# Side steps two at a time, block moves on two queues, and memory blocks split later, in a two-layer hybrid encoder trunk

## The chip, the core and the metric

The kernel runs on one core of a Trainium2 chip. The metric is the device time of one execution in microseconds (us). Each timed result is a median over runs of the same program; one further execution is recorded by the hardware profiler, and the rows below come from that one. The engines carry the profile's names: PE is TensorE (PEld its weight load), DVE is VectorE, ACT is ScalarE, POOL is GpSimd, SP is SyncE, which does nothing here but issue DMAs.

## The reference

x (256 tokens x 2048) goes through two layers. A layer normalizes x, projects it to 15,944 columns, and splits these into four branches of 512 columns (4 heads of 128) and their gates:

```python
h = rms_norm(x, norm_g); u = h @ w_in                                  # 2048 -> 15944
y_a = sparse_index_attention(norm(a_q), norm(a_k), a_v, a_qi, a_ki, a_wi)   # 8 index heads, top 64 keys
y_b = head_rms_norm(retention(rope(b_q), rope(b_k) * HD ** -0.5, b_v))
y_c = head_rms_norm(hgrn2(f, c_i, c_q))                               # f = lb + (1 - lb) * sigmoid(c_f)
m_k, m_v = halves of mem @ w_mem_kv                                   # mem: 256 x 2048
y_m = memory_attention(norm(m_q), norm(m_k), m_v)
merged = sum_n sigmoid(gate_n) * ((y_n * silu(z_n)) @ w_branch[n])    # 512 -> 2048, n = a, b, c, m
x = x + merged @ w_out
```

Everything is float32.

## The kernel before, in words

**The weight stream.** All weights, 336 tiles in the fixed order of `gemm_plan`, pass once through the core. A tile holds four blocks of 128 rows by (mostly) 512 columns, 1 MB. `load` has SP fetch a tile into `raw` (four buffers). `split_weights` takes half a tile (a half slab): ACT casts it to `whi` (L223), DVE subtracts to get the rest `wlo` (L224), and when a tile's second half is split, the next load is issued (L230). In `gemms` a half slab meets two blocks of the left operand, itself split into a high and a low part, in 12 products: high by high, high by low, low by high (L249 to L251) for two blocks and two halves of the 256 rows. There are 672 half slabs. Four pairs `whi`, `wlo` exist, so splits are written up to four half slabs ahead of the products.

**The side work.** Everything between the large products (norms, attention, retention, recurrence, transposes, the splitting of a left operand) is written as generators, the tasks of the class `Stream`. A `yield` ends a side step; a step that cannot go on gives BLOCKED. After the 12 products of each half slab `pump` (L113) runs at most one side step, that of the first task in line that can move. Where a product needs a task's result, `finish` (L123) runs that task to its end first, with no half slab between its steps. All this happens when the program is built: it decides the order in which each engine gets its instructions. Engines then run in that order and wait for each other by semaphores.

**The moves.** A 128 x 128 transpose is done by `fold` (L286): DVE transposes 32 x 32 blocks inside (tile names end in i), then 16 DMAs put the blocks in place, all on GpSimd's queue (L300). `tick` (L108), the first thing in `pump`, issues up to four moves per half slab; three half slabs after the last one the task goes on (L311). There are 44 such tiles, 704 moves.

**The start.** The left operand of the first 64 half slabs is the memory (mem transposed, four blocks `memr`, split to `memh` and `meml`), for the keys `mk` and values `mv` of both layers. The loop at L575 to L596 loads and splits the four blocks among the first weight tiles. The task `constants` (L603) loads the blocks of x transposed (`xr`, L613) and scales them with `split_scaled` (four activations on ACT each, L274), then loads x itself (`xs`, L619) for the norm.

**The places named below.** `bw` is a branch's product with its output weights, in the order c, a, m, b (L739); before it the branch's transposed output is cast (L266: `bnh` for c and b, `ah`, `mh`). `ixrp` are the index scores of branch a (L458), from the transposed index queries `ixqt` and keys `ixkt`. `bk` is the key of branch b, rotated on DVE in `rope_t` (L479 to L492). PSUM has two tiles for side work (`PB`) beside two for the stream.

Of the kernel before, what the change touches and what calls it, by code (L numbers as in the profile page):

```python
# [89 lines left out]
MOVES = 4  # L90


class Stream:
    def __init__(self):
        self.loaded = self.cut = self.used = self.ticks = self.idle = 0
        self.raw, self.parts, self.tasks, self.moves = deque(), deque(), [], deque()
# [10 lines left out]

    def tick(self):  # L108
        self.ticks += 1
        for _ in range(min(MOVES, len(self.moves))):  # L110
            self.moves.popleft()()

    def pump(self):  # L113
        self.tick()
        for t in list(self.tasks):
            moved = t.step()
            if t.done:
                self.tasks.remove(t)
            if moved:
                return True  # L120
        return False
# [43 lines left out]
def trunk(ctx: ExitStack, tc: tile.TileContext, x, xt, memt, ng, qkg, hg, lbl, win, wmem, wbr, wout,  # L165
# [120 lines left out]
    def fold(cuts, nb, name):  # L286
        inner = G([128, nb, 128], name + "i")
        at = 0
        for shape, src in cuts:
            n = int(np.prod(shape))  # L290
            part = inner[:, at:at + n, :]
            if len(shape) == 2:
                part = part.rearrange("p (a b) c -> p a b c", a=shape[0])
            ve.transpose(part, src)
            at += n
        yield from stream.rest(1)
        whole = G([128, nb, 128], name)

        def move(a, b):
            po.dma_start(whole[b, :, a], inner[a, :, b])  # L300

        cut = [slice(32 * i, 32 * i + 32) for i in range(4)]
        left = [(a, b) for a in cut for b in cut]

        def moved():
            move(*left.pop())

        stream.moves.extend([moved] * 16)
        while left:
            yield BLOCKED  # L310
        yield from stream.rest(3)  # L311
        return whole
# [56 lines left out]
    def head_norm(ps, zs, g, name):  # L369
        v = ps.rearrange("p (a d) -> p a d", a=8)  # L370
        zg = G([128, 2, 512], name + "zg")
        ve.tensor_tensor(zg, zs, g[:, None, :].to_broadcast([128, 2, W]), op=OP.mult)
        sq = G([128, 8, 128], name + "sq")
        ac.activation(sq, v, AF.Square)
        yield
        ss = SM(8, name + "ss")
        ve.reduce_sum(ss, sq, axis=AX.X)
        r = rsq(ss, 8, 1.0 / HD, name)
        yield
        y1 = G([128, 8, 128], name + "y1")  # L380
        ve.tensor_mul(y1, v, bc(r, HD))
        y = G([128, 2, 512], name + "y")
        ve.tensor_tensor(y, y1.rearrange("p (t h) d -> p t (h d)", t=2), zg, op=OP.mult)
        yield
        return (yield from branch_t(y, name))

    def attend(box, names, keys, name):
# [6 lines left out]
        for t in range(2):  # L394
            nk = keys[t]
            nb = nk // 128
            lg = PB(f"{name}lg{t}")[:, :4 * nk].rearrange("p (h s) -> p h s", h=4)
# [3 lines left out]
            if masks is not None:  # L401
                lm = G([128, 4, nk], f"{name}lm{t}")
                ve.tensor_add(lm, lg, masks[t][:, None, :].to_broadcast([128, 4, nk]))
                lg = lm
            mx = SM(4, f"{name}mx{t}")
# [6 lines left out]
            for h in range(4):  # L412
                ac.activation(p[:, h, :], lg[:, h, :], AF.Exp, bias=nm[:, h:h + 1], scale=ISQ,
                              accum_out=sm[:, h:h + 1])
            yield
# [5 lines left out]
            yield  # L421
            ov = PB(f"{name}ov{t}")[:, :512].rearrange("p (h d) -> p h d", h=4)
# [6 lines left out]
            ve.tensor_mul(on, ov, bc(rc, HD))  # L429
            zs = yield from wait_for(box, names[3])  # L430
# [5 lines left out]
    def selection(qi0, qi1, name):  # L436
# [11 lines left out]
        for t in range(2):  # L448
# [3 lines left out]
            for g in range(8 // per):  # L452
                yield
                ps = PB(f"{name}rp{t}{g}").rearrange("p (h s) -> p h s", h=per)
# [6 lines left out]
                ac.activation(rl, ps, AF.Relu, scale=NID ** -0.5)  # L461
                for h in range(g * per, g * per + per):
# [48 lines left out]
    def retention_scores(qt, kt, name):  # L511
        p0 = PB(name + "s0").rearrange("p (h t) -> p h t", h=4)
# [3 lines left out]
        ve.tensor_mul(s0, p0, csb[:, C_D:C_D + 1024].rearrange("p (h t) -> p h t", h=4))  # L516
        yield
        p1 = PB(name + "s1")[:, :512].rearrange("p (h t) -> p h t", h=4)
# [3 lines left out]
        ve.tensor_mul(s1, p1, csb[:, C_D + 1024:C_D + 1536].rearrange("p (h t) -> p h t", h=4))  # L522
        return (lambda h: s0[:, h, 0:128]), (lambda h: s0[:, h, 128:256]), (lambda h: s1[:, h, :])

    def hgrn_scores(uf, uq, lb, olb, name):
# [10 lines left out]
        yield  # L536
        ps = PB(name + "dg").rearrange("p (g t) -> p g t", g=8)
# [4 lines left out]
        ve.tensor_mul(a, ps, ident[:, None, :].to_broadcast([128, 8, 128]))  # L542
        tot = f.rearrange("p h t -> p (h t)")
        for i, m in enumerate(LEVELS):
            nb = 64 // m
            yield
            yield from stream.rest(1)
            ps = PB(f"{name}l{i}")[:, :512]
            for g in range(8):
# [7 lines left out]
                ps.rearrange("p (b j) -> p b j", j=m))  # L557
            tv = tot.rearrange("p (b two) -> p b two", two=2)
# [8 lines left out]
        yield  # L567
        ps = PB(name + "x")[:, :512].rearrange("p (h t) -> p h t", h=4)
# [3 lines left out]
        ac.copy(ax, ps)  # L572
        return (lambda h: a[:, 2 * h, :]), (lambda h: ax[:, h, :]), (lambda h: a[:, 2 * h + 1, :])

    memx = []  # L575
    for b in range(4):
        raw = G([128, 4, 256], "memr")
        hi = G([128, 4, 256], "memh", F32R)
        lo = G([128, 4, 256], "meml", F32R)
        for k0, k1 in [(0, 1), (1, 2), (2, 4)] if b == 0 else [(0, 4)]:  # L580
            if b == 0 and k0 == 0:
                part = load(True)
                part(0, 1)
            sy.dma_start(raw[:, k0:k1, :], memt[:, 4 * b + k0:4 * b + k1, :])
            if b == 0:
                for k in range(max(k0, 1), k1):
                    part(k, k + 1)
            ac.copy(hi[:, k0:k1, :], raw[:, k0:k1, :])
            ve.tensor_sub(lo[:, k0:k1, :], raw[:, k0:k1, :], hi[:, k0:k1, :].bitcast(F32))
            if b == 0 and k0 > 0:  # L590
                split_weights(True)
        memx.append((hi, lo))
        if stream.loaded < RAW:
            load()
        if b >= 2 and len(stream.parts) < HL:
            split_weights()  # L596
# [72 lines left out]
    for l in range(L):  # L669
# [8 lines left out]
        def mixed(scores, v, z, g, name):  # L678
# [3 lines left out]
            yield  # L682
            return (yield from head_norm(mix_values(sc, vt, name), zs, g, name + "n"))
# [37 lines left out]
        def merged(acc, d):  # L721
            if d == 3:
                yield
                u = turned_at_once(acc, "mgp")
            else:
                u = yield from transposed(acc, "mgp")
# [20 lines left out]
        def turned(c, xc, nssq, l=l):  # L747
            if c >= 2:
                yield
                u = turned_at_once(xc, "xp")  # L750
            else:
                u = yield from transposed(xc, "xp")
            r = split_scaled(u, ngs[:, l + 1, 4 * c:4 * c + 4], xtp, "xt", f"x1{c}")
            for t in range(2):
# [67 lines left out]
```

## Time and profile before

| | |
|---|---|
| timed, median of 3 runs | 1927.73 us (1927.24 to 1927.80) |
| the profiled execution | 1934.95 us, span of its instructions 1933.2 us |
| busy share: PE, DVE, ACT, POOL | 98%, 58%, 45%, 23% |
| mean granted clock of TensorE | 0.99 of 2.4 GHz |
| DMA: hardware queues, software queue (GpSimd's) | 52.8%, 5.6% of 16 engines' span |

The page cuts the span in 40 slices; a digit is the busy share, or the granted clock, in tenths:

```profile
PE   6999999999979999999999999999997999999999
PEclk8999999999989999999999999999998999999999
POOL 0323055056251001010120306406623101001000
```

TensorE is below nine tenths in slices 1, 12 and 31; its clock is lower in the same ones. A row of a timeline reads: start in us from the span's start, duration, engine, line, operation, output<-inputs, shape, count, and in brackets the idle time before it with what ended it.

### The profile page before, as it was taken

The numbers are of one execution on the slowest core, as the hardware profiler recorded it, in microseconds if no ns is written. First come the engines' busy times: TensorE is split into PE (matmuls) and PEld (weight loads), VectorE is DVE, ScalarE is ACT, GpSimd is POOL, SyncE is SP. The second block draws the span as 40 slices with busy tenths as digits, with TensorE's granted clock in tenths as the row PEclk, the third lists the DMA queues.
The fourth block names the chain that finished last, engine by engine and source line by source line (L and its number), as shares of the span: only waits on it lengthen the run. The fifth ranks groups of instructions, "written<-read, shape, count | busy, mean of one in ns | idle before, by whom it ended". The sixth has DMA issues, their size and how long they took to land.

```text
span 1933.2 us, 22621 instructions
## 1 busy us (share of the span) xinstructions
PE 1888.2 (98%) x8736; PEld 1576.7 (82%) x8736; DVE 1129.6 (58%) x1204; ACT 864.2 (45%) x995; POOL 437.6 (23%) x729
## 2 busy tenths in 40 slices
PE   6999999999979999999999999999997999999999
PEld 5888987888868888888888898888886888888887
DVE  5645765766655555555555577677564545555554
ACT  4644354445434444444454434454453444444442
POOL 0323055056251001010120306406623101001000
PEclk8999999999989999999999999999998999999999
DMA  7765556567465556565565546646755656556553
GB/s 294 264 222 174 186 189 190 191 201 210 163 182 197 191 193 204 195 206 196 188 203 207 167 173 205 212 180 204 230 167 162 202 192 204 195 196 207 195 196 110
DMA packets 76139, 379.18 MB, mean 196 GB/s; under 512 B 17536, under 2 KB 18944, under 8 KB 35072
## 3 DMA queue, kind: packets, MB, share of 16 engines
q1 hardware_dynamic: 53504, 355.94, 52.8%
q0 software_dynamic: 22528, 21.80, 5.6%
q8 instruction: 68, 1.11, 0.2%
q14 instruction: 39, 0.32, 0.1%
HBM read 353.82 MB, written 2.10 MB: 184 GB/s over the span
## 4 chain that ended last, share of the span: by engine, by line
PE 94%; DMA 3%; POOL 1%; issue 0%; DVE 0%; SPq 0%; ACT 0%; DVEq 0%; ACTq 0%; POOLq 0%
PE u L249 23%; PE u L250 23%; PE u L251 22%; PE bw L249 3%; PE bw L251 3%; PE bw L250 3%; PE wo L251 3%; PE wo L250 3%; PE wo L249 3%; PE cl L551 1%; PE mv L250 1%; PE mv L251 1%; PE mv L249 1%; DMA memr<-in_memt 1%; PE mk L251 1%; PE mk L250 1%
## 5 line engine op out<-in xcount | busy, mean ns | idle before, releaser
L224 DVE TENSOR_TENSOR wlo<-raw,whi 128x1024 fp32r<-128x1024 f32 (+2 forms) x674 | 804.1, 1198 | 670.2 <-ACT whi L223 669.2
L223 ACT CAST whi<-raw 128x1024 fp32r<-128x1024 f32 (+2 forms) x674 | 694.9, 1033 | 951.4 <-PE u L251 738.2
L300 POOL DMA_DIRECT2D mgp<-mgpi x96 | 55.2, 583 | 493.4 <-ACT whi L223 294.7
L249 PE MATMUL u<-whi,x02h 128*128 128x512 f32 (+2 forms) x256 | 99.4, 388 | 0.0
L249 PE MATMUL u<-whi,x12h 128*128 128x512 f32 (+2 forms) x256 | 99.0, 387 | 0.0
L249 PE MATMUL u<-whi,x00h 128*128 128x512 f32 (+2 forms) x256 | 98.9, 386 | 0.0
L249 PE MATMUL u<-whi,x10h 128*128 128x512 f32 (+2 forms) x256 | 98.9, 386 | 0.0
L249 PE MATMUL u<-whi,x11h 128*128 128x512 f32 (+2 forms) x256 | 98.6, 385 | 0.0
L249 PE MATMUL u<-whi,x01h 128*128 128x512 f32 (+2 forms) x256 | 98.6, 385 | 0.0
L249 PE MATMUL u<-whi,x03h 128*128 128x512 f32 (+2 forms) x256 | 98.5, 385 | 0.0
L249 PE MATMUL u<-whi,x13h 128*128 128x512 f32 (+2 forms) x256 | 98.5, 385 | 0.0
L250 PE MATMUL u<-wlo,x02h 128*128 128x512 f32 (+2 forms) x256 | 98.4, 384 | 0.0
L251 PE MATMUL u<-whi,x02l 128*128 128x512 f32 (+2 forms) x256 | 98.3, 384 | 0.0
L250 PE MATMUL u<-wlo,x12h 128*128 128x512 f32 (+2 forms) x256 | 98.2, 383 | 0.0
L251 PE MATMUL u<-whi,x12l 128*128 128x512 f32 (+2 forms) x256 | 98.2, 383 | 0.0
L251 PE MATMUL u<-whi,x11l 128*128 128x512 f32 (+2 forms) x256 | 98.2, 383 | 0.0
L250 PE MATMUL u<-wlo,x00h 128*128 128x512 f32 (+2 forms) x256 | 98.1, 383 | 0.0
L250 PE MATMUL u<-wlo,x10h 128*128 128x512 f32 (+2 forms) x256 | 98.1, 383 | 0.0
L251 PE MATMUL u<-whi,x10l 128*128 128x512 f32 (+2 forms) x256 | 98.1, 383 | 0.0
L251 PE MATMUL u<-whi,x00l 128*128 128x512 f32 (+2 forms) x256 | 98.1, 383 | 0.0
L250 PE MATMUL u<-wlo,x11h 128*128 128x512 f32 (+2 forms) x256 | 98.1, 383 | 0.0
L250 PE MATMUL u<-wlo,x13h 128*128 128x512 f32 (+2 forms) x256 | 98.1, 383 | 0.0
(369 smaller groups left out, 3883.5 us busy)
## 6 DMA issues: line engine op xcount, KB each, us to landing
raw<-in_win SPq DMA_DIRECT2D x240, 1024.0 KB, 4.9
raw<-in_wbr SPq DMA_DIRECT2D x32, 1024.0 KB, 4.8
raw<-in_wout SPq DMA_DIRECT2D x32, 1024.0 KB, 4.9
raw<-in_wmem SPq DMA_DIRECT2D x15, 1024.0 KB, 5.1
raw<-in_win SPq DMA_DIRECT2D x8, 656.0 KB, 4.0
raw<-in_win SPq DMA_DIRECT2D x8, 512.0 KB, 3.5
mgp<-mgpi POOLq DMA_DIRECT2D x96, 32.0 KB, 4.1
xr<-in_xt SPq DMA_DIRECT2D x4, 512.0 KB, 6.0
```

The source lines that it names most:

```text
L223: ac.copy(hi[:, a:b, :], r)
L224: ve.tensor_sub(lo[:, a:b, :], r, hi[:, a:b, :].bitcast(F32))
L249: te.matmul(ps[:, t, :n], ah[:, 2 * j + k, c], wh[:, k, :], start=first, stop=False)
L250: te.matmul(ps[:, t, :n], ah[:, 2 * j + k, c], wl[:, k, :], start=False, stop=False)
L251: te.matmul(ps[:, t, :n], al[:, 2 * j + k, c], wh[:, k, :], start=False, stop=last)
L300: po.dma_start(whole[b, :, a], inner[a, :, b])
L551: te.matmul(ps[:, g * 64:g * 64 + 64].rearrange("p (b j) -> p b j", j=m), kd[:, g // 2, c], qd[:, g // 2, c].rearrange("p (b two j) -> p b ...
```

## The change

After each half slab up to two side steps are taken instead of one (a task gives one step per turn, so they come from two tasks). Counters for PSUM keep two side tiles open at most: a step that would take a third is BLOCKED (`bank` ahead of each such tile, `free` behind its last reader; both act only while the program is built). Of the moves that `tick` issues, every second goes to SP's queue. At the start the loads are written ahead of the splits, one more weight tile is issued before the small loads, and memory blocks 1 to 3 are split as whole blocks by three tasks, which come up after half slabs 1, 4 and 7.

```diff
-MOVES = 4
+MOVES, STEPS, BANKS = 4, 2, 2
...
+    def bank(self):
+        while self.banks == BANKS:
+            yield BLOCKED
+        self.banks += 1
+    def free(self):
+        self.banks -= 1
     def tick(self):
         self.ticks += 1
-        for _ in range(min(MOVES, len(self.moves))):
-            self.moves.popleft()()
+        for i in range(min(MOVES, len(self.moves))):
+            self.moves.popleft()(i)
     def pump(self):
         self.tick()
+        n = 0
         for t in list(self.tasks):
-            moved = t.step()
+            n += t.step()
             if t.done:
                 self.tasks.remove(t)
-            if moved:
-                return True
-        return False
+            if n == STEPS:
+                break
...
-        def move(a, b):
-            po.dma_start(whole[b, :, a], inner[a, :, b])
+        def move(q, a, b):
+            q.dma_start(whole[b, :, a], inner[a, :, b])
...
-        def moved():
-            move(*left.pop())
+        def moved(i):
+            move((po, sy)[i % 2], *left.pop())
...
@     def retention_scores(qt, kt, name):
+        yield from stream.bank()
         p0 = PB(name + "s0").rearrange("p (h t) -> p h t", h=4)
...
         ve.tensor_mul(s0, p0, csb[:, C_D:C_D + 1024].rearrange("p (h t) -> p h t", h=4))
+        stream.free()
...
-    memx = []
-    for b in range(4):
-        raw = G([128, 4, 256], "memr")
...
+    def split_later(raw, after, name):
+        yield from stream.rest(after)
+        return split(raw, gen, "g", name)
+
+    part = load(True)
+    part(0, 1)
+    raw = G([128, 4, 256], "memr")
+    for k0, k1 in [(0, 1), (1, 2), (2, 4)]:
+        sy.dma_start(raw[:, k0:k1, :], memt[:, k0:k1, :])
+        for k in range(max(k0, 1), k1):
+            part(k, k + 1)
+    memr = [raw] + [G([128, 4, 256], "memr") for b in range(1, 4)]
+    load()
+    sy.dma_start(memr[1], memt[:, 4:8, :])
+    load()
+    load()
+    for b in (2, 3):
+        sy.dma_start(memr[b], memt[:, 4 * b:4 * b + 4, :])
+    hi = G([128, 4, 256], "memh", F32R)
+    lo = G([128, 4, 256], "meml", F32R)
+    split_pieces(hi, lo, raw, [(0, 1), (1, 2)])
+    split_weights(True)
+    split_pieces(hi, lo, raw, [(2, 4)])
+    split_weights(True)
+    split_weights()
+    split_weights()
+    memx = [(hi, lo)] + [stream.add(split_later(memr[b], 3 * b - 2, "mem")) for b in range(1, 4)]
```

What this moves on the engines, as the order of their instructions shows it:

ACT at the start, before; `memh` are casts of memory blocks, `whi` casts of weights (the first two half slabs in two pieces each), `x00h` the scaling of the first x block:

```order
L588 CAST memh<-memr 128x256 x2
L223 CAST whi<-raw 128x512 x2
L588 CAST memh<-memr 128x512
L223 CAST whi<-raw 128x512 x2
L588 CAST memh<-memr 128x1024 x2
L223 CAST whi<-raw 128x1024
L588 CAST memh<-memr 128x1024
L223 CAST whi<-raw 128x1024 x5
L274 ACTIVATE x00h<-xr,ngs 128x256 x4
```

The same place after:

```order
L604 CAST memh<-memr 128x256 x2
L231 CAST whi<-raw 128x512 x2
L604 CAST memh<-memr 128x512
L231 CAST whi<-raw 128x512 x2
L231 CAST whi<-raw 128x1024 x3
L274 CAST memh<-memr 128x1024
L231 CAST whi<-raw 128x1024 x3
L274 CAST memh<-memr 128x1024
L282 ACTIVATE x00h<-xr,ngs 128x256 x4
```

The casts of blocks 1 to 3 stand among or behind weight casts that they stood ahead of: block 1 has the weights of five half slabs ahead of it instead of two, and between block 0 and the scaling of x stand six casts of whole weight halves and two blocks instead of six and three; the last block follows the second x block.

ACT before the product of branch m in layer 0, before; `mh` is the cast of m, `bnh` that of b, `mp` the exponentials of m, each `gate` belongs to one `bw`:

```order
L223 CAST whi<-raw 128x1024
L374 ACTIVATE bnsq<-bo 128x1024
L223 CAST whi<-raw 128x1024 x5
L736 ACT_TABLE_LOAD
L736 ACTIVATE gate<-u,rs0r 128x512 x2
L223 CAST whi<-raw 128x1024 x10
L736 ACTIVATE gate<-u,rs0r 128x512 x2
L266 CAST mh<-mpt 128x1024
L266 CAST bnh<-bnpt 128x1024
L223 CAST whi<-raw 128x1024 x10
L736 ACTIVATE gate<-u,rs0r 128x512 x2
```

After, the same stretch:

```order
L231 CAST whi<-raw 128x1024 x7
L776 ACTIVATE gate<-u,rs0r 128x512 x2
L231 CAST whi<-raw 128x1024 x4
L274 CAST bnh<-bnpt 128x1024
L231 CAST whi<-raw 128x1024 x4
L274 CAST mh<-mpt 128x1024
L231 CAST whi<-raw 128x1024 x2
L776 ACTIVATE gate<-u,rs0r 128x512 x2
L231 CAST whi<-raw 128x1024 x10
L776 ACTIVATE gate<-u,rs0r 128x512 x2
```

The cast of m stood directly behind the gate of its own product, with no weight cast between; it now stands behind the cast of b, which followed it before, two weight casts ahead of the gate of branch a and twelve ahead of its own.

SP in layer 0 around the index branch, before; `raw` are weight tiles:

```order
L670 DMA hgs<-in_hg 128x1024
L211 DMA raw<-in_win 128x2048 x11
L211 DMA raw<-in_win 128x1024 x4
L211 DMA raw<-in_win 128x1312 x4
L211 DMA raw<-in_win 128x2048 x44
```

After, the stretch with the index keys `ixkt`, the output of branch c (`cnpt`) and the index queries `ixqt`:

```order
L219 DMA raw<-in_win 128x2048 x8
L308 DMA ixkt<-ixkti 32x2x32 x4
L219 DMA raw<-in_win 128x2048
L308 DMA ixkt<-ixkti 32x2x32 x4
L219 DMA raw<-in_win 128x2048
L308 DMA cnpt<-cnpti 32x8x32 x4
L219 DMA raw<-in_win 128x2048
L308 DMA cnpt<-cnpti 32x8x32 x4
L219 DMA raw<-in_win 128x2048
L308 DMA ixqt<-ixqti 32x8x32 x4
L219 DMA raw<-in_win 128x2048
L308 DMA ixqt<-ixqti 32x8x32 x4
```

SP had only weight loads there; now four moves of a tile stand between two of them, and GpSimd has the other eight of each sixteen.

## Rows read from the trace of the kernel before

**Rows 1.** the page: busy us, share of the span, instructions by engine

```profile
PE 1888.2 (98%) x8736; PEld 1576.7 (82%) x8736; DVE 1129.6 (58%) x1204; ACT 864.2 (45%) x995; POOL 437.6 (23%) x729
```

**Rows 2.** what TensorE waited for: us in total, times, longest

```profile
PE bw L249 <- ACT mh L266: 20.7, 2, 10.7
PE mv L249 <- ACT whi L223: 9.3, 1, 9.3
...
PE ixrp L458 <- DMA akpt<-akpti: 4.0, 1, 4.0
```

**Rows 3.** TensorE's timeline, layer 0, around m's product: start us, us, what

```profile
557.92 0.39 PE L249 MATMUL u<-whi,x03h 128*128 128x512 f32 x1
...
576.60 0.39 PE L249 MATMUL bw<-whi,mh 128*128 128x512 f32 x1
```

**Rows 4.** the same in layer 1

```profile
1466.31 0.39 PE L249 MATMUL u<-whi,x13h 128*128 128x512 f32 x1
...
1484.39 0.39 PE L249 MATMUL bw<-whi,mh 128*128 128x512 f32 x1
```

**Rows 5.** by stretch, third and fourth half slab: busy us, then PEclk

```profile
23.10:29.50 6.40, 5.75 (x13) 4.18 (x14) 5.92 (x6) 3.72 (x4) 0.00 (x0) 0.50 0.27 79
```

**Rows 6.** timeline, layer 0, GpSimd's moves of m and ScalarE's cast of m

```profile
563.77 3.45 POOL L300 DMA_DIRECT2D mpt<-mpti  x6 [0.16 <-issue]
570.45 1.04 ACT L266 CAST mh<-mpt 128x1024 fp32r<-128x1024 f32 x1 [7.40 <-DMA mpt<-mpti]
```

**Rows 7.** TensorE at the first index scores, layer 0, then layer 1

```profile
312.82 0.39 PE L249 MATMUL u<-whi,x01h 128*128 128x512 f32 x1
...
319.73 2.27 PE L458 MATMUL ixrp<-ixkt,ixqt 64*128 64x128 f32 x16 [4.03 <-DMA akpt<-akpti]
...
325.41 0.39 PE L249 MATMUL u<-whi,x02h 128*128 128x512 f32 x1
...
1227.05 0.39 PE L249 MATMUL u<-whi,x11h 128*128 128x512 f32 x1
...
1233.81 0.39 PE L249 MATMUL u<-whi,x12h 128*128 128x512 f32 x1
```

**Rows 8.** GpSimd's timeline, the last moves of the index queries

```profile
311.32 2.31 POOL L300 DMA_DIRECT2D ixqt<-ixqti  x4 [2.05 <-issue]
```

**Rows 9.** ScalarE's timeline at the start

```profile
10.99 0.62 ACT L223 CAST whi<-raw 128x512 fp32r<-128x512 f32 x1 [0.75 <-DMA raw<-in_wmem]
17.25 1.04 ACT L588 CAST memh<-memr 128x1024 fp32r<-128x1024 f32 x1 [5.64 <-DMA memr<-in_memt]
...
33.44 1.71 ACT L274 ACTIVATE x00h<-xr,ngs 128x256 fp32r<-128x256 f32 x4
```

**Rows 10.** TensorE's timeline, two half slabs in step

```profile
32.28 0.39 PE L249 MATMUL mk<-whi,memh 128*128 128x512 f32 x1
...
35.00 0.39 PE L249 MATMUL mk<-whi,memh 128*128 128x512 f32 x1
```

**Rows 11.** SP's issues at the start (SPq: its sequencer)

```profile
4.98 2.11 SPq L584 DMA_DIRECT2D memr<-in_memt  x1
...
45.70 0.33 SPq L211 DMA_DIRECT2D raw<-in_wmem  x1
46.07 0.65 SPq L619 DMA_DIRECT2D xs<-in_x  x1
```

**Rows 12.** the page: queues with their share; issues with us to landing

```profile
q0 software_dynamic: 22528, 21.80, 5.6%
...
mgp<-mgpi POOLq DMA_DIRECT2D x96, 32.0 KB, 4.1
xr<-in_xt SPq DMA_DIRECT2D x4, 512.0 KB, 6.0
```

**Rows 13.** VectorE's timeline around the rotation of bk

```profile
427.43 0.74 DVE L488 SCALAR_TENSOR_TENSOR bka<-u,rs0r,csb 128x512 f32<-128x512 f32 x1
...
433.14 1.22 DVE L224 TENSOR_TENSOR wlo<-raw,whi 128x1024 fp32r<-128x1024 f32 x1
```

More of the change, by code (lines that the diff above doesn't have):

```diff
@@ L404, in attend @@
                 lg = lm
+                stream.free()
             mx = SM(4, f"{name}mx{t}")
@@ L414, in attend @@
                               accum_out=sm[:, h:h + 1])
+            if masks is None:
+                stream.free()
             yield
@@ L421, in attend @@
             yield
+            yield from stream.bank()
             ov = PB(f"{name}ov{t}")[:, :512].rearrange("p (h d) -> p h d", h=4)
@@ L453, in selection @@
                 yield
+                yield from stream.bank()
                 ps = PB(f"{name}rp{t}{g}").rearrange("p (h s) -> p h s", h=per)
@@ L511, in retention_scores @@
     def retention_scores(qt, kt, name):
+        yield from stream.bank()
         p0 = PB(name + "s0").rearrange("p (h t) -> p h t", h=4)
@@ L516, in retention_scores @@
         ve.tensor_mul(s0, p0, csb[:, C_D:C_D + 1024].rearrange("p (h t) -> p h t", h=4))
+        stream.free()
         yield
+        yield from stream.bank()
         p1 = PB(name + "s1")[:, :512].rearrange("p (h t) -> p h t", h=4)
@@ L536, in hgrn_scores @@
         yield
+        yield from stream.bank()
         ps = PB(name + "dg").rearrange("p (g t) -> p g t", g=8)
@@ L547, in hgrn_scores @@
             yield from stream.rest(1)
+            yield from stream.bank()
             ps = PB(f"{name}l{i}")[:, :512]
@@ L567, in hgrn_scores @@
         yield
+        yield from stream.bank()
         ps = PB(name + "x")[:, :512].rearrange("p (h t) -> p h t", h=4)
@@ L572, in hgrn_scores, with split_pieces @@
         ac.copy(ax, ps)
+        stream.free()
         return (lambda h: a[:, 2 * h, :]), (lambda h: ax[:, h, :]), (lambda h: a[:, 2 * h + 1, :])
-    memx = []
-    for b in range(4):
-        raw = G([128, 4, 256], "memr")
[L578 to L587, printed above, removed]
+    def split_pieces(hi, lo, raw, cuts):
+        for k0, k1 in cuts:
             ac.copy(hi[:, k0:k1, :], raw[:, k0:k1, :])
             ve.tensor_sub(lo[:, k0:k1, :], raw[:, k0:k1, :], hi[:, k0:k1, :].bitcast(F32))
[L590 to L596, printed above, removed]
+    def split_later(raw, after, name):
[24 more added lines that the diff above has]
+    memx = [(hi, lo)] + [stream.add(split_later(memr[b], 3 * b - 2, "mem")) for b in range(1, 4)]
     box = {}
@@ L682, in mixed @@
             yield
+            yield from stream.bank()
             return (yield from head_norm(mix_values(sc, vt, name), zs, g, name + "n"))
@@ L723, in merged @@
                 yield
-                u = turned_at_once(acc, "mgp")
-            else:
-                u = yield from transposed(acc, "mgp")
+                yield from stream.bank()
+                r = split(turned_at_once(acc, "mgp"), gen, "g", f"mg{d}")
+                stream.free()
+                return r
+            u = yield from transposed(acc, "mgp")
             return split(u, gen, "g", f"mg{d}")
@@ L749, in turned @@
                 yield
+                yield from stream.bank()
                 u = turned_at_once(xc, "xp")
```

9 lines of the change are left out of this document (8 added, 1 removed).

## The prediction, made before the changed kernel ran

> **What bounds the kernel now.** I read the page's busy shares first, then the list of what TensorE waited for, then the timeline around each wait, and last the order of the instructions. TensorE is busy for 98% of the span [rows 1], nearly all of it in the 672 half slabs of the weight stream: 12 products each, one half slab every 2.72 us (32.28 to 35.00 in [rows 10]). That pace isn't touched by the change: it has the same products in the same number. What can be won is only where TensorE stands still or runs at its lower clock, and the list of waits has four such places [rows 2]: the start (9.28 us), the index scores of layer 0 (4.03), and the first product of branch m with its output weights in each layer (10.74 and 10.00, one row with count 2). Each costs more than the wait, since TensorE comes back at its lower level: after the wait at the start it was granted 0.50 of the clock, 1.2 of 2.4 GHz, for 6.4 us [rows 5]. So I take each loss from the first product before the wait to the first at full pace behind it.
>
> **The products of branch m, both layers: 25.9 us.** In layer 0, 24 products run from 557.92 to 576.60, 18.68 us; at full pace two half slabs take 5.44, so 13.24 are lost [rows 3]. In layer 1 it is 1466.31 to 1484.39, 18.08, so 12.64 [rows 4]. The cause stands on the other engines: the block moves of m (tile mpt) are still being issued by GpSimd at 567.2, and ScalarE waits 7.40 us for them before it can cast m [rows 6]. The program had run out of half slabs there: it issues 12 of the 16 moves, the cast and the subtraction after the last half slab before the product. In the new order the cast of m stands 12 half slabs (32.6 us) ahead of the product, in both layers, because two side steps after each half slab let m run beside the other branches. Even if its moves landed 10 us late, TensorE would not notice. What is late next there is branch b, whose cast stands 26 half slabs ahead of its product. I count the whole 25.9.
>
> **The index scores of layer 0: 5.8 us.** The half slab with them and the next take 12.59 us in layer 0 (312.82 to 325.41), and 6.76 in layer 1, where nothing is waited for (1227.05 to 1233.81): 5.83 lost [rows 7]. The wait ended with the last moves of the query tile ixqt. GpSimd was behind: at 3.45 us for six moves [rows 6] the four moves after each half slab take it 2.3 of 2.72 us, and it stood still besides, as the 2.05 us before the last four moves of ixqt show [rows 8]. Now SP issues half of them, the scores come 8 half slabs earlier in the stream, and their last moves are due for issue four half slabs (10.9 us) before them, as they were, but on two queues, neither of which lags. I count the whole 5.8.
>
> **The start: 5 us, between 0 and 11.3.** ScalarE works in order. Before, it casts memory blocks 1, 2 and 3 among the first weights, so the third half slab's weights wait behind blocks that TensorE doesn't need yet: the cast of block 1 stood 5.64 us for its landing at 17.25, and block 2 comes later still [rows 9]. Now the second weight tile's two casts come first. When does that tile land? Between 10.99 (first weights complete) and 17.25 there landed two weight tiles and block 1, 2.5 MB, so 2.5 us per MB [rows 9]. The second tile lands at 10.99 + 2.5 = 13.5, its cast takes 1.04, and the third half slab starts at 14.6 instead of 23.1. Its second product waits 1.0 for the subtraction (1.22 us, as in [rows 13]). Six half slabs later, at 14.6 + 1.0 + 16.3 = 31.9, TensorE wants half slab 8. In the kernel before it had it at 32.28 + 4 x 2.72 = 43.2 [rows 10], a lead of 11.3 us: the upper end.
> But in front of that half slab's cast stands the scaling of the first x block, four activations of 1.71 us together [rows 9]. It waits for that block, and SP issues it behind the seventh weight tile. By the same 2.5 us per MB it lands at 10.99 + 20.2 = 31.2 (six weight tiles behind the first, three memory blocks and itself, 8 MB, and 0.2 us for the 0.09 MB of four small loads). So the cast ends at 31.2 + 1.7 + 1.0 = 33.9, the subtraction at 35.2: TensorE waits 2.0 us and then 1.0, and leads by 8.3. From there on the x loads set a loop. A load is issued when a pair of half slabs is split, it takes 6.0 us to land [rows 12], then come 1.71 for scaling, 1.04 and twice 1.22 for the next splits, with 0.35 for the weight load ahead of it on SP: 11.5 us for four half slabs that TensorE does in 10.88. The square of the memory keys also moves in there (as many columns as a cast, 1.0 us). I give back 3.3 more over half slabs 12 to 22 and keep 5. The lower end is 0: before, the scaling began at 33.44 [rows 9] and casts were ahead, so all of the lead could be eaten by x loads that land no earlier than they did.
>
> **What the change adds.** No product, cast or subtraction is new; block 0 is still split in three pieces. The bookkeeping of PSUM banks runs when the program is built and has no instruction. Of 704 moves 352 go to SP's queue. What one takes SP no row shows; the nearest with 256 pieces is the x load, 0.65 us, the shortest possible is a weight load's 0.33, the longest issue in the trace 2.11 [rows 11]. I take 0.65: with two moves and half a weight load SP is busy 1.5 of 2.72 us. In bytes the moves are small: the software queue takes 5.6% of 16 engines for all 704 [rows 12], 0.15 us each on every engine. A move's landing can be earlier or later by a weight load (2.5 us); consumers stand at least three half slabs (8.2 us) behind the last move, against 4.1 us to land [rows 12], so I count 0.
> VectorE gets steps of two branches between two splits. Its worst place now is around half slab 135: a transpose and a maximum, two more transposes and four splits (eight passes over 1024 columns, each taken as a subtraction's 1.22: 9.8) and the rotation of bq (at most 5.7, as that of bk from 427.43 to 433.14 in [rows 13]), 15.5 in four half slabs of 10.9 us. It falls at most 4.6 us behind; splits stand ahead by three half slabs less cast and subtraction, 8.2 - 2.3 = 5.9 us. So I count 0, with 1.3 us of cover left; if it fails, the price is some 2 us a layer. The rotation alone stood between two splits before with no wait of TensorE among [rows 2].
>
> **The sum.** 25.9 + 5.8 + 5 = 36.7 us. Against the profiled execution's own 1934.95 (span 1933.2 and 1.75 around it) that gives 1898.2. The median of the timed runs is 7.2 us lower than the profiled one. If the new kernel is lower by the same, it takes 1891.0; if the 7.2 us are waits that are shorter without the profiler, the gain is smaller by them and it takes 1898.2. I forecast the middle, 1894.
>
> **The rivals.**
> (a) The start keeps all of its lead (11.3): 1888. For it: the weights alone would allow it. Against: the x block's place in the queue. 0.12.
> (b) The start gives everything back, or the index scores still wait: 1894 + 5 to 6 = 1900. For the second: GpSimd still issues half, and a wait of a queue for its own landings is in [rows 8]. 0.16. The Trainium skill (DMA: Bandwidth & Descriptors, Issuing engines are not separate DMA queues) says that a second issuing engine saves only issue time, since all transfers run on the same engines; by it the wait for the scores would shrink by GpSimd's issue time alone, which is what I have counted. No row here shows moves on two queues.
> (c) Moves on SP's queue land behind whole weight loads. The x loads, which stand behind a weight load, need 6.0 us [rows 12]; with a second weight load ahead (2.5) and 0.6 for the issue a move needs 9.1 us against 8.2 of cover: 0.9 late at six products a layer that moves feed, 11 us, 1905. Against: the transfers of both queues already share the wires. 0.12. The Trainium skill (DMA: Bandwidth & Descriptors, Queues, rings and completion order) has each DMA engine serve its queues in turn, packet by packet, and one queue in the order of its ring; by that a move of GpSimd can pass a weight load and one of SP can't, which is this rival. No row of the kernel before has a move on SP's queue.
> (d) The other side: an issue on SP is so long that the weights come late. At 2.11 us [rows 11] SP needs 4.4 us per half slab of moves and falls back 1.7. Moves follow without a break over stretches of 20 and some 36 half slabs a layer; weights stand about 12 us ahead; 22 + 49 us a layer, 142 in all: 2036. It turns slower than before from 1.64 us an issue. Against: 0.65 for the x load. 0.04.
> (e) The change doesn't do what it says: the steps of m come early but a product placed ahead of its operand stops TensorE for as long, and the time stays near 1925. Against: the distances between steps of one branch are not shorter than before. 0.04.
>
> **How the numbers follow.** The forecast has 0.52 and by itself 1889 to 1900 (the 7.2 us either way, and 2 us at the start). Adding (a), (b) and most of (c) gives 1884 to 1908, with about 0.17 outside: (d), (e), the far part of (c) and a start better than (a). Less than 0.2%, 3.9 us, can't be told from no change here. Slower holds (d) and a little of (e), 0.05; the same 0.03; faster 0.92.
>
> **What would show it.** Right: no wait of TensorE over 1 us after half slab 22; the third half slab at about 14.6 us and waits of 1 to 3.5 us at half slabs 8 to 22 that end with x loads; granted clock 1.00 in the slices with both m products; SP's issue of a move under 1 us. Wrong: waits of TensorE on transposed tiles (c), SP issues over 1.6 us with TensorE waiting for weight casts (d), or a start that ends with the kernel before (b).

## The result, and the profile after

The changed kernel takes 1905.20 us (median of 4 runs, 1904.43 to 1905.74) against 1927.76 of the kernel before on the same chip: ratio 0.9881, interval 0.9864 to 0.9899, 22.6 us less. The forecast was 1894, its range 1884 to 1908. The profiled execution takes 1905.74 us, span 1903.9.

The page's engine line and slices of the changed kernel:

```profile
PE 1885.3 (99%) x8736; PEld 1574.5 (83%) x8736; DVE 1127.7 (59%) x1204; ACT 863.5 (45%) x995; POOL 238.7 (13%) x377
...
PE   7999999999999999999999999999999999999999
...
PEclk9999999999999999999999999999999999999999
```

Slices 12 and 31 are full and at full clock now; only slice 1 is low, and TensorE's busy time fell by just 2.9 us against [rows 1]. The list of what TensorE waited for:

```profile
PE mk L257 <- ACT whi L231: 10.5, 3, 5.5
PE mk L258 <- DVE wlo L232: 3.0, 4, 1.0
PE mv L258 <- DVE wlo L232: 0.6, 1, 0.6
```

All of these lie in the first 31 half slabs. The rows of the products of m and of the index scores in [rows 2] are gone. At m, layer 0, ScalarE's timeline (the casts of b and m), then TensorE's: the first product of the last half slab before m's (number 187, counted from 0 as everywhere here) and that of half slab 189, where the 24 products of [rows 3] end:

```profile
517.66 1.05 ACT L274 CAST bnh<-bnpt 128x1024 fp32r<-128x1024 f32 x1 [2.67 <-DMA mpt<-mpti]
...
525.77 1.05 ACT L274 CAST mh<-mpt 128x1024 fp32r<-128x1024 f32 x1
```

```profile
554.54 0.39 PE L257 MATMUL u<-whi,x03h 128*128 128x512 f32 x1
...
559.98 0.39 PE L257 MATMUL bw<-whi,mh 128*128 128x512 f32 x1
```

m was cast 31.5 us before it was wanted (525.77 against 554.54 + 2.72 = 557.3), and the 24 products that took 18.68 us in [rows 3] take 5.44. The index scores stand behind half slab 99 instead of 107 and wait for nothing:

```profile
293.51 0.39 PE L257 MATMUL u<-whi,x01h 128*128 128x512 f32 x1
...
296.32 1.16 PE L474 MATMUL ixrp<-ixkt,ixqt 64*128 64x128 f32 x16
```

The start is another matter. ScalarE's timeline: the first cast of the second weight tile, the scaling of the first x block, and the squares of x (`xs`) that waited longest, one for each of three of its four loads (that of the second load waited 0.58 us):

```profile
11.94 2.00 ACT L231 CAST whi<-raw 128x1024 fp32r<-128x1024 f32 x2 [1.89 <-DMA raw<-in_wmem]
...
31.35 1.70 ACT L282 ACTIVATE x00h<-xr,ngs 128x256 fp32r<-128x256 f32 x4 [9.47 <-DMA xr<-in_xt]
...
54.21 0.63 ACT L661 ACTIVATE xsq<-xs 128x512 f32<-128x512 f32 x1 [2.09 <-DMA xs<-in_x]
...
67.87 0.64 ACT L661 ACTIVATE xsq<-xs 128x512 f32<-128x512 f32 x1 [4.71 <-DMA xs<-in_x]
...
75.28 0.63 ACT L661 ACTIVATE xsq<-xs 128x512 f32<-128x512 f32 x1 [4.17 <-DMA xs<-in_x]
```

TensorE at the start of half slabs 2, 8, 22 and 24, from the timeline:

```profile
13.80 0.39 PE L257 MATMUL mv<-whi,memh 128*128 128x512 f32 x1
...
34.04 0.50 PE L257 MATMUL mk<-whi,memh 128*128 128x512 f32 x1 [3.33 <-ACT whi L231]
...
78.61 0.50 PE L257 MATMUL mk<-whi,memh 128*128 128x512 f32 x1 [1.61 <-ACT whi L231]
...
88.20 0.39 PE L257 MATMUL mv<-whi,memh 128*128 128x512 f32 x1
```

Half slab 2 starts at 13.80 instead of 23.09 and half slab 7 at 27.83, a lead of 12.6 us over [rows 10] counted on in steps of 2.72. Then the lead goes: at half slab 8 TensorE waits 3.33 us, since the cast stands behind the scaling that waited 9.47 us for x. At 24 the kernel before is 1.5 us ahead (32.28 + 20 x 2.72 = 86.68 against 88.20), at 31 2.4. By stretch (length in us, busy us of PE, PEld, DVE, ACT, POOL with their counts, PEclk, DMA share, GB/s): half slab 8; half slab 21 with the wait behind it; 22 and 23; 24 to 27:

```profile
34.00:39.30 5.30, 4.50 (x13) 3.41 (x14) 5.28 (x8) 5.23 (x8) 0.00 (x0) 0.68 0.38 106
74.10:78.60 4.50, 2.90 (x13) 2.06 (x11) 1.50 (x12) 2.53 (x7) 0.71 (x1) 1.00 0.97 312
78.60:88.20 9.60, 8.61 (x24) 6.64 (x25) 6.13 (x7) 3.84 (x4) 4.51 (x7) 0.64 0.92 310
88.20:98.00 9.80, 9.80 (x45) 8.12 (x44) 1.34 (x2) 5.21 (x7) 2.70 (x5) 1.00 0.19 52
```

After each of the two longer waits the granted clock is 0.68 and 0.64 on the mean, and the half slab behind a wait takes 5.2 and 6.3 us instead of 2.72 (0.8 and 1.0 of it a second wait, for VectorE). Bytes are not short over the whole of the start: the DMA engines are busy for 0.97 of one stretch and 0.19 of the one after next.

### The profile page after: what moved, and what is told of

The parts are those of the page before. It is cut to its first block, busy times and chain, and to the rows that moved or that the text cites. A ratio compares the mean times of both kernels' runs of the same rounds, so it can differ in the third digit from the quotient of the medians.

```text
span 1903.9 us, 23024 instructions
## 1 busy us (share of the span) xinstructions
PE 1885.3 (99%) x8736; PEld 1574.5 (83%) x8736; DVE 1127.7 (59%) x1204; ACT 863.5 (45%) x995; POOL 238.7 (13%) x377
## 4 chain that ended last, share of the span: by engine, by line
PE 94%; DVE 0%; issue 0%; DVEq 0%
PE u L257 24%; PE u L258 24%; PE u L259 24%; PE wo L258 3%; PE wo L259 3%; PE bw L258 3%; PE bw L259 3%; PE bw L257 3%; PE wo L257 3%; PE cl L575 1%; PE mov L439 0%; PE mlg L409 0%; PE ixrp L474 0%; PE aov L439 0%; PE alg L409 0%; PE cdg L562 0%
## 5 line engine op out<-in xcount | busy, mean ns | idle before, releaser
L308 POOL DMA_DIRECT2D mgp<-mgpi x48 | 27.6, 582 | 588.7 <-ACT whi L231 293.3
L258 PE MATMUL u<-wlo,x03h 128*128 128x512 f32 (+2 forms) x256 | 98.2, 383 | 0.0
L258 PE MATMUL u<-wlo,x01h 128*128 128x512 f32 (+2 forms) x256 | 98.2, 383 | 0.0
L259 PE MATMUL u<-whi,x01l 128*128 128x512 f32 (+2 forms) x256 | 98.1, 383 | 0.0
```

The source lines that it names most:

```text
L258: te.matmul(ps[:, t, :n], ah[:, 2 * j + k, c], wl[:, k, :], start=False, stop=False)
L259: te.matmul(ps[:, t, :n], al[:, 2 * j + k, c], wh[:, k, :], start=False, stop=last)
L308: q.dma_start(whole[b, :, a], inner[a, :, b])
```

## The experiments

The runs were made on several chips, on which the kernel before has medians of 1927.8 to 1934.2 us, single executions from 1927.2 to 1937.9. So ratios are to the kernel before on the same chip, and times are set beside each other where the chip was the same (e1 to e3; e4 to e7; e8 to e10).

**e0: the kernel before, once more.** No edit.

> The kernel before, profiled a second time. My sum was made against a profiled execution of 1934.95 us, 7.2 above the timed median, and I took half of that as waits that the profiler lengthens. If so, this profile is near 1935 again, with waits of 10 us at the first products of m. Rival: the 7.2 us are how that one execution fell (waits that end with moves differ from run to run); then this profile is near 1928, and the waits for m or for the index scores are shorter by about 7 us in sum.

1929.51 us, span 1927.7. What TensorE waited for, the index scores of layer 0 with the product ahead of them, and GpSimd's last moves of the index queries:

```profile
PE bw L249 <- ACT mh L266: 20.9, 2, 10.9
PE mv L249 <- ACT whi L223: 7.5, 1, 7.5
```

```profile
313.89 0.39 PE L251 MATMUL u<-whi,x01l 128*128 128x512 f32 x1
314.21 1.16 PE L458 MATMUL ixrp<-ixkt,ixqt 64*128 64x128 f32 x16
```

```profile
301.66 2.31 POOL L300 DMA_DIRECT2D ixqt<-ixqti  x4 [0.94 <-DMA ixqt<-ixqti]
305.16 2.31 POOL L300 DMA_DIRECT2D ixqt<-ixqti  x4 [1.19 <-issue]
```

The rival holds. The two waits at m are there as in [rows 2]; that at the index scores ([rows 7]) isn't. GpSimd was through with the queries at 307.47, in [rows 8] at 313.63, of which 1.4 us come from the start; it stood still less between its moves. The two executions of the same program stand 7.26 us apart at half slab 120: 1.42 from the start, 5.84 from the scores. So the 5.8 us are not in every execution. How often they come, two traces can't tell. But of the 44 timed executions of the kernel before that belong to e0 to e11, 14 lie more than 4 us above the lowest on their chip (up to 10.5); so do 6 of the 12 of e7, the one kernel below that also has one step and all moves on GpSimd; in all other kernels the largest distance is 4.2. That the long ones are those with this wait is likely and not shown. Against this one the changed kernel gains 23.8 us of span: 14.5 and 13.2 at m (half slabs 187 to 200 take 35.36 us instead of 49.81, 505 to 520 take 40.80 instead of 54.02), and 3.9 lost at the start.

**e1: the old start, with two side steps and moves on two queues.** The block of the start (L602 on) replaced by that of the kernel before.

> The changed kernel with the start (loads and splits of the memory blocks) as before the change. In the changed kernel the start lost 2.4 us by half slab 31 where I forecast a gain of 5. Theory A: the new start won 12.6 us by half slab 7 and gave them back because loads of x come late for ScalarE; the old start, which has casts ahead there, is as it was, and the time is 1905.2 - 2.4 = 1902.8. Rival B: the second side step puts the work on the memory keys between the loads of x whatever the start; then the old start loses 2 to 8 us on top of its 13 and the time is 1905 to 1911, with waits of TensorE at half slabs 18 to 24.

1902.68 us, ratio 0.9845 (0.9827 to 0.9864). No wait between half slabs 3 and 30; the third half slab's 7.9 us is back:

```profile
PE mv L257 <- ACT whi L231: 7.9, 1, 7.9
```

Theory A's number. B, as put there (the second step spoils any start), falls; it is the two together that lose, as e2 shows. The loads of x are no further from their use in this program, yet ScalarE waits for none of the eight; it waits for TensorE to free a buffer instead. One such wait, and the first square of x:

```profile
53.54 1.05 ACT L231 CAST whi<-raw 128x1024 fp32r<-128x1024 f32 x1 [1.66 <-PE mk L259]
...
55.45 0.64 ACT L651 ACTIVATE xsq<-xs 128x512 f32<-128x512 f32 x1
```

From the issue of that load (45.37) to its use are 10.1 us; in the changed kernel, where TensorE is ahead and ScalarE has no such slack, 6.2 (48.02 to 54.21). So a distance in half slabs is not yet a time.

**e2: one side step until the x loads are through.**

```diff
-            if n == STEPS:
+            if n == (STEPS if self.wide else 1):
...
         lower_bounds()
+        stream.wide = True
```

> The changed kernel, but only one side step per half slab until the task that loads x is through. The work on the memory keys then comes behind all loads of x, as before the change. Theory B (the second step spoils the start): the losses at half slabs 18 to 24 go (the lead falls there from 6.3 to -1.5 us): 1905.2 - 8 = 1897. Theory A (a load of x every two half slabs, 6 us to land behind a weight load that waits for its buffer, is too tight by itself): TensorE waits there nearly as long, 1902 to 1906.

1898.68 us, ratio 0.9824 (0.9805 to 0.9843): near theory B's 1897, outside A's range, and 4.0 less than e1 on its chip. Up to half slab 26 TensorE has no wait behind the first ones and keeps a lead of 12.2 us over the first profile, though ScalarE still waits 0.65 to 3.7 us at all eight loads of x. So with two half slabs between load and use ScalarE waits, but it takes the second step's work on the memory keys in between (a square, a sum, a product, a transpose, moves) to make TensorE wait. (One step also puts the use of x one half slab later where a memory block is split. That concerns the first two loads; for the other six ScalarE still waited 0.9 to 2.9 us, at no cost to TensorE.) e7, with one step throughout, has similar waits of ScalarE (0.6 to 3.6 us) and no loss before half slab 28. At half slab 27, 5.5 us of what was won are lost in another way. GpSimd's timeline and TensorE's wait:

```profile
78.67 3.97 POOL L667 CAST msb<-csb 128x512 uint8<-128x512 f32 x7 [5.57 <-DMA csb<-in_cf]
82.59 1.64 POOL L292 TENSOR_TENSOR mk0r<-mk0v,nhalf 128x8 f32<-128x8 f32 x1
```

```profile
86.69 0.50 PE L259 MATMUL mv<-wlo,memh 128*128 128x512 f32 x1 [3.66 <-DVE wlo L233]
```

GpSimd works in order: the root of the memory keys' norm (`mk0r`) stood behind seven casts of masks that waited 5.57 us for the second constants load, VectorE waited for it, and with it the next weights.

**e3: four half slabs between each load of x and its use.**

```diff
-            yield
-            yield
+            yield from stream.rest(4)
```

in both loops of `constants`.

> The changed kernel with four half slabs instead of two between a load of x and its first use (all eight loads). Theory A: ScalarE no longer waits for x, the waits of TensorE at half slabs 8 to 22 go, most of the 12.6 us lead at half slab 7 is kept: 1905.2 - 2.4 - 10 to 12 = 1891 to 1893. Rival: the start is bound by bytes (weights, memory and x share the engines); then the same bytes land as late, the lead falls as before, 1900 to 1905.

1891.88 us (1891.13 to 1892.09), ratio 0.9788 (0.9770 to 0.9806): theory A's number, 10.8 less than e1 and the lowest median of all; the rival falls. TensorE's waits, complete, and two squares of x on ScalarE, without idle time before them:

```profile
PE mk L257 <- ACT whi L231: 5.5, 1, 5.5
PE mv L258 <- DVE wlo L232: 0.6, 1, 0.6
```

```profile
70.72 0.63 ACT L659 ACTIVATE xsq<-xs 128x512 f32<-128x512 f32 x1
...
81.61 0.62 ACT L659 ACTIVATE xsq<-xs 128x512 f32<-128x512 f32 x1
```

ScalarE waits only at the first load of x (3.60 us) and the last (3.13). The lead of 11.7 us at half slab 7 is still 11.7 at half slab 64. Two more things change with it: as a `rest` takes no side step, the memory keys come forward (the work is the same, in another order), and the loads of x come half as often. The three are not told apart.

**e4 to e7: the parts apart.** All moves on GpSimd (e4); in addition the old start, so the second step alone (e5); one step and the old start, so the moves alone (e6); one step and all moves on GpSimd, so the new start alone (e7). The edits:

```diff
-            move((po, sy)[i % 2], *left.pop())
+            move(po, *left.pop())
...
-MOVES, STEPS, BANKS = 4, 2, 2
+MOVES, STEPS, BANKS = 4, 1, 2
```

> The changed kernel with all block moves on GpSimd's queue. The second profile of the kernel before had no wait at the index scores of layer 0, so the 5.8 us that I counted for them may belong to one execution. Theory A: with GpSimd alone the scores are in time in nearly every execution, and the second queue is worth 0 to 1 us: 1904.5 to 1906.5. Rival, my prediction's step: GpSimd is behind, the scores or other products of layer 0 and 1 wait for moves, 4 to 6 us more: 1909 to 1912. A third: moves on SP's queue go out in pieces of 128 bytes (144128 packets in place of 53504) and hinder the weights; then this kernel is faster, 1903 or less.

> The second side step alone: start as before the change, all moves on GpSimd. Theory A: the second step alone makes the whole gain at the products of m (25.9 us by the first profile, 27 against the second): 1902 to 1904, as with moves on both queues and the old start (1902.7). Rival: without SP's share the moves lag, 1907 to 1909.

> The moves on two queues alone: one side step, start as before. The products of m still come right behind 12 moves and a cast; half of these moves leave GpSimd, 6 x 0.58 = 3.5 us less in each layer: 7 us less than the kernel before, ratio 0.996. Rival: SP's moves stand behind weight loads that wait for a buffer, and nothing is won at m, ratio 0.999 to 1.001. By my prediction's step on the index scores another 5.8 us would go, ratio 0.993.

> The new start alone: one side step, all moves on GpSimd. The work on the memory keys then comes behind the loads of x. Theory A by the run with one step at the start (6.6 us ahead of the kernel before from half slab 28 on, 1.4 of them the first profile's own): 5 us less than the kernel before, ratio 0.997 to 0.998. Rival: the loads of x alone eat the lead, ratio 0.999 to 1.001.

| run | second step | new start | SP moves | us | ratio, interval |
|---|---|---|---|---|---|
| e5 | yes | | | 1903.58 | 0.9862 (0.9847 to 0.9877) |
| e6 | | | yes | 1922.66 | 0.9960 (0.9946 to 0.9973) |
| e7 | | yes | | 1924.90 | 0.9983 (0.9967 to 0.9998) |
| e1 | yes | | yes | 1902.68 | 0.9845 (0.9827 to 0.9864) |
| e4 | yes | yes | | 1907.83 | 0.9884 (0.9869 to 0.9899) |
| changed kernel | yes | yes | yes | 1905.20 | 0.9881 (0.9864 to 0.9899) |

Each part gains alone: the second step 25.6 us (from the before runs' 1929.18), the moves on SP 6.5, the new start 4.3 (by its interval 0.4 to 6.4). e5 and e6 came as first forecast; e7's 0.9983 lies between its two forecasts. The gains don't add. With the second step there is no wait at m left for SP's moves to shorten: in e6, where there is, the waits are

```profile
PE bw L257 <- ACT mh L274: 15.6, 2, 8.3
```

against 20.9 in e0, the 12 moves being issued by two engines. And the new start turns from 4.3 us won to 4.2 lost once the second step is there (e4 against e5, same chip). For e4 neither number came as it stands: 1907.83 lies between theory A's 1906.5 and the rival's 1909; but by its ratio it would take 1905.4 on the chip of the first result, theory A's. Behind half slab 31 it has no wait at all, so the index scores were in time without SP. What it loses stands at the start again (ScalarE):

```profile
93.77 1.15 ACT L360 ACTIVATE mk0pt<-mk0pt,qks 128x1024 f32<-128x1024 f32 x1 [8.50 <-DMA mk0pt<-mk0pti]
```

Eight moves of the memory keys stood behind the casts of masks on GpSimd; in the changed kernel SP had half of these. From half slab 24 to 31 e4 loses 2.8 us against the changed kernel, having gained 1.4 before. That is all that the second queue gives beside the second step, and by the ratios it can't be told from nothing.

**e8: three half slabs between load and use of x.** As e3 with `stream.rest(3)`.

> The changed kernel with three half slabs (8.2 us) between a load of x and its first use, in place of two (5.4) or four. A load of x takes 5.8 to 7.5 us. Theory A (what counts is whether the distance covers the landing): three cover it, 1891 to 1894, as with four. Rival: the gain of four came from spreading the bytes, then three give about half of it, 1897 to 1900.

1895.16 us, ratio 0.9812 (0.9789 to 0.9836): between the two theories' numbers, and by the ratios not told apart from e3. ScalarE still waits, 2.4 to 4.4 us at the squares of the first three loads of `xs`. A load is due when its step is written, but SP issues it behind a weight load that waits for VectorE to free its buffer; that wait comes on top of the landing. Once SP waited for itself (waits of SP, half slabs 15 to 27):

```profile
SPq L219 <- DVE wlo L232: 19.5, 5, 7.4
SPq L655 <- DMA raw<-in_wmem: 2.5, 1, 2.5
```

These waits at the squares cost TensorE nothing: its lead over the first profile is 11.4 us from half slab 12 to 28 (e3's 11.7). What it lost stands elsewhere: 1.3 us at half slabs 8 to 11, behind the first x block (ScalarE waits 6.39 us for it, in e3 3.60); 1.0 at 30; and 1.9 at 38 and 39, where ScalarE waits for moves of the second memory keys that stood behind casts of masks on GpSimd:

```profile
115.68 1.15 ACT L360 ACTIVATE mk1pt<-mk1pt,qks 128x1024 f32<-128x1024 f32 x1 [8.17 <-DMA mk1pt<-mk1pti]
```

**e9: four half slabs, all moves on GpSimd.** The edits of e3 and e4.

> Four half slabs between a load of x and its use, and all block moves on GpSimd. With the start repaired, is the second queue worth anything? If not: 1891 to 1893, as with both queues (1891.9). If GpSimd alone is late with moves in some place: 1894 to 1898. If moves on SP's queue hinder the weights by their small packets: 1890 or less.

1892.21 us, ratio 0.9802 (0.9779 to 0.9825), as e3: with the start repaired the second queue is worth nothing that can be measured, and harms nothing.

**e10: GpSimd issues the loads of x.**

```diff
-            sy.dma_start(raw, xt[:, 4 * b:4 * b + 4, :])
+            po.dma_start(raw, xt[:, 4 * b:4 * b + 4, :])
...
-            sy.dma_start(xs[:, :, c * 512:c * 512 + 512], x[:, :, c * 512:c * 512 + 512])
+            po.dma_start(xs[:, :, c * 512:c * 512 + 512], x[:, :, c * 512:c * 512 + 512])
```

> The changed kernel with the eight loads of x issued by GpSimd instead of SP, still two half slabs ahead of their use. GpSimd has nothing else to do there, so it issues them at once, and they don't stand behind a weight load that waits for its buffer. If it was the distance from issue to use that counts, no use of x waits after the start, but 4 MB (10 us at 2.5 us per MB) now land among the first weights: the second weight tile comes up to 10 us later, and TensorE starts as late as in the kernel before without losing more: 1900 to 1905. If the position on SP counts nothing and the work on the memory keys is the cause, the waits at half slabs 18 to 24 stay: 1908 to 1915.

1902.85 us, ratio 0.9858 (0.9834 to 0.9882), in the first theory's range. Six of the eight loads went out within 5 us and landed among the first weights. The second weight tile's cast, at 11.94 in the changed kernel:

```profile
19.55 1.99 ACT L231 CAST whi<-raw 128x1024 fp32r<-128x1024 f32 x2 [3.21 <-DMA raw<-in_wmem]
```

Half slab 3 starts 9.8 us later than there, and from then up to half slab 26 TensorE waits for nothing, with the second step and the work on the memory keys in place (ScalarE waits for one load of x, the seventh, 3.75 us; behind 26, at late moves of the memory keys, 4.3 us are lost). The number is the theory's, but the run doesn't decide for it: TensorE starts nearly as late as in e1, where SP's loads, two half slabs ahead, made nobody wait either. That the loss took both, loads too close to their use and the work that the second step puts between, rests on e2 (keys out of the way, loads as close: no loss up to half slab 26) and on e3 (keys among the loads, loads further apart: none), with the early start under it.

**e11: three half slabs, all moves on GpSimd.** The edits of e8 and e4.

> Three half slabs between a load of x and its use, and all block moves on GpSimd. With moves on SP, the third load of xs waited on SP 2.5 us for the landing of a weight load, since four moves of the memory keys stood ahead of it and SP has at most eight DMAs under way. Theory: without moves on SP the loads of x go out earlier and three half slabs do as four: 1891.5 to 1893. Rival: three are short by themselves (ScalarE waited 2.4 us for the first xs already): 1894 to 1896.

1898.07 us, ratio 0.9816 (0.9800 to 0.9832), that of e8 by ratio (its chip runs the kernel before in 1934.20). The theory falls: TensorE's lead at half slab 64 is 5.5 us, against 11.7 with four half slabs, and without moves on SP ScalarE still waited 3.42, 2.09 and 4.43 us for x. So moves on SP are not why three half slabs leave ScalarE waiting. As in e8 these waits cost TensorE nothing (its lead is 10.5 from half slab 12 to 28); 3.8 us go at half slabs 38 and 39, where the moves of the second memory keys, all behind GpSimd's casts of masks, cost more (ScalarE):

```profile
117.03 1.15 ACT L360 ACTIVATE mk1pt<-mk1pt,qks 128x1024 f32<-128x1024 f32 x1 [8.53 <-DMA mk1pt<-mk1pti]
```

## Why the prediction was right and where it failed

**The number.** 1905.2 lies in the range and 11.2 us above the forecast; the gain is 22.6 us where 33.7 was forecast, and the forecast's own stretch, 1889 to 1900, missed. The range reached that far for rival (c), moves that land too late on SP's queue, whose number is 1905; that didn't happen, so the agreement is luck. The 11.2 us are two steps, both below: 7.4 at the start (5 won counted, 2.4 lost measured), and some 4 for taking the middle of 1891.0 and 1898.2 (which is 1894.6) where the first profile's whole 7.2 us above the median should have been left out of the gain.

**The products of m, 25.9 us: right.** Measured by the same half slabs 13.24 and 12.64 against the first profile, 14.5 and 13.2 against e0, all of it from the second step (e5). Distance, price and the absence of a later wait were as worked out.

**The index scores, 5.8 us: failed.** "I count the whole 5.8" took a wait of one execution for one that the median holds. [Rows 7] and [rows 8] were read rightly, but how long GpSimd stands still between moves differs from run to run (what the 2.05 us of [rows 8] waited for, no row says; I called it a wait for landings under (b)), and e0 has no wait there. The sign was in the numbers: the profiled execution was 7.2 us above the median. I offered two readings, both about the profiler, and took the middle; the second, that the gain is smaller by it, has the right number for another reason. Against e0 the first profile has 5.84 more at the scores and 1.42 at the start, and 1.8 less at m.

**The start, 5 us: right to half slab 8, then failed.** The cast of the second tile came at 11.94 (13.5 worked out), the x block at 31.3 (31.2), TensorE's wait ended at 34.04 (33.9), and its second product started at 35.30 (35.2). From there I gave it a lead of 8.3 us; measured are 9.1 at the start of half slab 8 and 6.6 at that of 9, since TensorE ran it at the lower clock (5.22 us), which I had counted at m and not here. The step that failed is "I give back 3.3 more over half slabs 12 to 22 and keep 5": from half slab 9 to 31 it gave back 9.1. The loop was the one I named, loads of x that land after their use is due; its size was wrong, because I added to it one square of the memory keys and left out the sum, product, transpose and 16 moves that the second step puts there, and the clock behind each wait. The start came out at -2.4, rival (b), at -3.9 against e0. The signs named for "right" all came but one (15 of SP's 352 moves took over 1 us to issue), while the start was lost: waits of 1 to 3.5 us at half slabs 8 to 22 say nothing of what the half slabs behind them cost.

**What the change adds: right.** SP's issues of moves in layer 0:

```profile
288.53 2.83 SPq L308 DMA_DIRECT2D aqpt<-aqpti  x4
```

That is 0.71 us each; the median of all is 0.61, the longest 2.09 (worked with 0.65). No product waits for a move and none for weights behind half slab 31, so (c) and (d) did not come; the moves of `mgp` land 5.5 us after their issue on SP and 5.1 on GpSimd (median; 4.1 before), not the 9.1 of (c). As counted, VectorE's crowded place near half slab 135 cost nothing. By the first profile the sum is 25.9 + 5.8 - 2.4 = 29.3, and the two profiled executions differ by 29.2. The median moved by 22.6, near e0's ledger, 27.7 - 3.9 = 23.8 of span.

**The rule of the Trainium skill** that I weighed under (b) (DMA: Bandwidth & Descriptors, Issuing engines are not separate DMA queues): the runs agree with it. e9 against e3 gains nothing from the second issuing engine, as nothing waits for issue time there; e6, where the 12 moves ahead of m do, gains 5.9 us of span against e0 (6.5 by the medians on its own chip).

## What to carry to other kernels

Before a wait is counted as won, look whether it is in a second execution of the same kernel; a profile some microseconds above the median holds something that the median doesn't. A load needs a time to its use that covers its landing and the wait of its issue behind other loads' buffers, and that time is not fixed by the number of half slabs between: two were enough with the old start, where ScalarE waited for TensorE, and too few once the start was faster and the second step put more work between; four (10.9 us) were enough again. Whoever makes one engine faster or side work denser should look at each such distance anew, and price each wait of TensorE with the half slab at the lower clock behind it.

## What the runs showed of the hardware that was not expected

The same move is cut into more packets on SP's queue than on GpSimd's. The page's queues of the changed kernel:

```profile
q1 hardware_dynamic: 144128, 366.84, 59.2%
q0 software_dynamic: 11264, 10.90, 2.7%
```

Before, the software queue had 22528 packets for 704 moves, 32 each, and the hardware queue 53504; now the hardware queue has 90624 more for 352 moves, 257 each, and the share of the engines that it takes rose by 106 us of span, 0.30 us a move, twice the 0.15 of GpSimd's (estimates from these shares and [rows 12]). e9 against e3 shows no time for it here. An engine's own queue also holds it up: SP in e8 waited 2.5 us for the landing of a weight load before it could issue the next load of x, and GpSimd in e0 0.94 us for a move of its own. In e8 eight of SP's DMAs had not landed at that moment (issued from 63.50 to 69.62, the first landing at 72.70), and in no trace here does an engine have more than eight under way; what sets the eight is not shown.
